# A transformer block on one core: value tiles through other staging rooms, background loads on ScalarE's queue, additions ordered behind weight halves

## The chip, the cores and the metric

The kernel runs on one core of one Trainium2 chip. The metric is the device time of one execution in microseconds (us); lower is better. Times of several executions are given as a median. The profile and the trace come from one further execution, which has a time of its own.

The engines are named as the profile does: PE is TensorE with its matmuls, PEld its weight loads, DVE is VectorE, ACT is ScalarE, POOL is GpSimd, SP is SyncE. Each engine works through its own list of instructions in order. DMAs are issued by SP, ACT or POOL and run on 16 DMA engines.

## The reference

One layer on a sequence of 1024 tokens with 1024 channels, everything in float32:

```python
h = rmsnorm(x, g_pre_mix)
proj = h @ w_in                       # u_pool | q | k | v, 512 channels each
y_pool = multiscale_pool(u_pool, ...) @ w_br_pool   # trailing means of 2, 4, 8, 16 tokens
o_sb = stick_breaking_attention(q, k, v)            # 8 heads of 64, strictly causal
gates = sigmoid(h @ w_gate + b_gate)  # 2048 channels
merged = gates[:, :1024] * y_pool + gates[:, 1024:] * (o_sb @ w_br_sb)
x = x + rmsnorm(merged @ w_out, g_post_mix)
h2 = rmsnorm(x, g_pre_mlp)
ff = square(relu(h2 @ w_up)) @ w_down  # 4096 channels between
x = x + rmsnorm(ff, g_post_mlp)
```

## The kernel before

Each float32 factor is split into a high and a low part of a reduced format. A product is then three matmuls of 128 x 512 (L104 high by high, L105 and L106 with one low part each) into one PSUM bank. Weights are split by `split_weights` (L1112 to L1119): a cast on ACT gives the high half, a subtraction on DVE (L1118) the low half; `prep` (L64) does the same with L74 and L75. TensorE needs both halves.

The program is a row of phases. The scheduler of the tile framework merges what the code issues into one list for each engine, and `issue_after` makes one instruction be placed behind another.

**Projection** (`phase_project`, L620). The gate, q and k projections are made as 12 pairs of outputs (L485: gates 0 to 4, q 0, k 0, q 1, k 1, gates 5 to 7). A pair is made with 7 products of 12 matmuls in place of 8, so there are 84 products, and the q and k pairs are products 35 to 62. The products go to PSUM banks of three tags in turn, with 2, 2 and 3 banks, so that 7 can be in flight (L626). DVE and ACT read the products and combine them in tiles u, c11, v and c22 (L651 to L662). When one of the four results of a pair is complete, `result` (L521) finishes it. For a gate, ACT takes the sigmoid (L526) and issues the store (L527). For q and k, ACT casts the high part (L530) and DVE computes the low part (L531) into a room in SBUF (128 x 1024 elements), and POOL issues the stores to DRAM: four for a q tile (L538 and L536 twice each), two for a k tile (L536). The rooms are m0 and m1 in turn (`staged`, L517). A room is free again when the last store from it has landed.

**In the background** of the same products runs the generator `later` (L540). Each `yield` in it waits for the next product (`next(bg)`, L638); every sixth product takes one step more (L640, L641). It first loads the pooling weights (L547), then makes four pooling groups in the rooms m0 to m3: a load of u (L555), running sums on DVE, a matmul `dm`, an evacuation on ACT (L584) and DVE, two stores (L590). Then come eight value tiles: two loads of 256 KB `vpair` (L595), a difference on DVE (L599), a cast on ACT (L602), a residual on DVE (L603), a store of 512 KB (L604). Tile t takes two neighbouring rooms, `vpair` in m2 and `vs` in m3 for even t, m0 and m1 for odd t.

**Attention** (`phase_attention`, L899) takes the q, k and value tiles back from DRAM. SP issues the loads of the first two heads into m0 to m3 (`load_head`, L705 to L718).

**Post** (`phase_post`, L968): the second half of the out projection runs on TensorE (L104 to L106 with `mg_hi`, `mg_lo`). Beside it, `chain(h=0)` (L1014) makes the norm of the first half of the tokens: for each of 8 blocks of channels a scaling on DVE (L1037), an addition of the residual (L1041), a store (L1042) and a square for the next norm. For the second half (h = 1) these two instructions are ordered behind the last low half of `prep` (`last_lo`); for h = 0 they aren't.

**MLP** (`phase_mlp`, L1150). A first loop makes 32 outputs and stores them (`pscr`). Then 16 pairs of outputs are made with 5 products each (L1194 on). For each pair the weights' sums and halves are made one pair ahead (`pair_weights`, L1139: L1126 to L1136 sums, L1118 low halves). Two quarters, u and c11, come back from `pscr` on ACT's queue (`quarter`, L1180), and DVE adds them (L1205) before ACT takes the squared ReLU (L1154, L1155) and POOL stores it (L1156).

Of the kernel before, what the change touches and what calls it, by code (L numbers as in the profile page):

```python
# [19 lines left out]
F32 = mybir.dt.float32  # L20
# [12 lines left out]
P = 128  # L33
# [19 lines left out]
class Block:  # L53
# [486 lines left out]
    def later(self):  # L540

        nc = self.nc
        def whole(n, dt=F32, name="ps"):
            return self.mx.tile([P, 1024], dt, name=name, tag=f"m{n}")

        wm = whole(0)[:, :512].rearrange("p (g n) -> p g n", g=4)
        nc.gpsimd.dma_start(wm, self.wmix)  # L547
        wmh, wml = (self.rp.tile([P, 4, P], F32R, name=f"wm{n}", tag=f"rb{n}") for n in range(2))
        nc.scalar.copy(wmh, wm)
        nc.vector.tensor_sub(wml, wm, wmh.bitcast(F32))  # L550
        yield
        for g in range(4):
            iu = 3 * (g % 2)
            u = whole(iu, name="u")
            nc.gpsimd.dma_start(u, self.uscr[g])  # L555
            yield
            yield
            yield
            cur, n = u, 0
            for i in range(g + 1):  # L560
                sh = 1 << i
                n = 1 + i % 2
                nxt = whole(n, name="win")
                nc.vector.tensor_add(nxt[:, sh:], cur[:, sh:], cur[:, : 1024 - sh])
                nc.vector.tensor_copy(nxt[:, :sh], cur[:, :sh])
                cur = nxt
                yield
            w = 1 << (g + 1)
            nc.vector.scalar_tensor_tensor(
                out=cur[:, w:], in0=cur[:, w:], scalar=1.0 / w, in1=u[:, w:], op0=ALU.mult, op1=ALU.subtract  # L570
            )
            nc.vector.tensor_mul(cur[:, :w], cur[:, :w], self.rcnt[:, :w])
            nc.vector.tensor_sub(cur[:, :w], cur[:, :w], u[:, :w])
            yield
            sc = self.vt[:, V_PSC + g : V_PSC + g + 1]
            ph, pq = whole(3 - n, F32R, "ph"), whole(3 - iu, F32R, "pq")
            nc.scalar.copy(ph, cur)
            nc.vector.tensor_sub(pq, cur, ph.bitcast(F32))
            yield
            for h in range(2):  # L580
                c = slice(h * H, h * H + H)
                d = self.zps.tile([P, H], F32, name="dm", tag="o", bufs=1)
                self.mm3(d, [(wmh[:, g, :], wml[:, g, :], ph[:, c], pq[:, c])])
                nc.scalar.activation(cur[:, c].bitcast(F32R), d, AF.Copy, scale=sc)  # L584
                nc.vector.scalar_tensor_tensor(
                    out=u[:, c].bitcast(F32R), in0=d, scalar=sc, in1=cur[:, c], op0=ALU.mult, op1=ALU.subtract
                )
                yield
            for t, scr in zip((cur, u), self.yscr):
                nc.gpsimd.dma_start(scr[:, g, :], t)  # L590
        for t in range(NK):
            n = 2 * (t % 2 == 0)
            p = self.mx.tile([P, 2, H], F32, name="vpair", tag=f"m{n}")
            for j in range(2):
                nc.gpsimd.dma_start(p[:, j, :], self.vscr[t * P + j : t * P + j + P, :])  # L595
            yield
            yield
            e = p[:, 0, :]
            nc.vector.tensor_sub(e, e, p[:, 1, :])  # L599
            e = e.rearrange("p (h x) -> p h x", h=8)  # L600
            v = self.mx.tile([P, 8, P], F32R, name="vs", tag=f"m{n + 1}")
            nc.scalar.copy(v[:, :, 0:64], e)  # L602
            nc.vector.tensor_sub(v[:, :, 64:128], e, v[:, :, 0:64].bitcast(F32))  # L603
            nc.gpsimd.dma_start(self.sscr[t], v.rearrange("p h x -> p (h x)").bitcast(F32))  # L604
            yield

    def sum_pieces(self, behind, n):
        with self.tc.issue_after(behind.ins):
            for _ in range(n):
                next(self.wsums)  # L610
# [9 lines left out]
    def phase_project(self):  # L620
        tc, nc = self.tc, self.nc
# [3 lines left out]
        def part(name):  # L625
            return pw.tile([P, H], F32, name=name, tag=name, bufs=1 + (name == "u"))  # L626
# [6 lines left out]
        def product(w, at, name):  # L633
            pool, tag, n = next(banks)
            d = pool.tile([P, H], F32, name="sw", tag=tag, bufs=n)
            self.half(d, w, at, name)
            next(nxt, None)
            next(bg, None)  # L638
            c = next(count)
            if c % 6 == 5:  # L640
                next(bg, None)  # L641
            if c % 2 and c < 32:
                self.sum_piece_with(self.last_mm)
            return d

        for i, (kind, f1) in enumerate(self.PAIRS):
# [3 lines left out]
            u, c11, v, c22 = (part(n) for n in ("u", "c11", "v", "c22"))  # L650
# [27 lines left out]
        for h in range(2):  # L678
            c = slice(h * H, h * H + H)
# [334 lines left out]
    def chain(self, ch, h, mix, acc):  # L1014

        nc = self.nc
        xr = []
        for i, n in enumerate(("hi", "lo")):
            t = self.hp.tile([P, 4, H], F32, name=f"xr{h}_{n}", tag=f"t4_{n}")
# [12 lines left out]
        for e in range(8):  # L1032
            yield 6 + 3 * e
            m = mix[e]

            with self.tc.issue_after(self.last_lo) if h else contextlib.nullcontext():
                nc.vector.scalar_tensor_tensor(  # L1037
                    out=m, in0=m, scalar=self.gn[:, V_POST_MIX + e : V_POST_MIX + e + 1], in1=r,
                    op0=ALU.mult, op1=ALU.mult,
                )  # L1040
                nc.vector.tensor_add(m, m, xr[e])  # L1041
            nc.gpsimd.dma_start(self.xscr[h][e], m)  # L1042
            sq = tmp[:, e % 3, :] if e else acc2
            nc.scalar.activation(sq, m, AF.Square)
            if e:
                nc.vector.tensor_add(acc2, acc2, sq)
# [16 lines left out]
        t = [self.big.tile([P, NK, H], F32R, name=f"b{h}_{n}", tag=f"big_{n}{h}") for n in ("hi", "lo")]  # L1063
# [48 lines left out]
    def split_weights(self, src, pool, tag, bufs, room=1024):  # L1112
        nc = self.nc
        n = src.shape[-1]
        hi = pool.tile([P, room], F32R, name=f"{tag}hi", tag=f"{tag}hi", bufs=bufs)[:, :n]
        lo = pool.tile([P, room], F32R, name=f"{tag}lo", tag=f"{tag}lo", bufs=bufs)[:, :n]
        nc.scalar.copy(hi, src)  # L1117
        nc.vector.tensor_sub(lo, src, hi.bitcast(F32))  # L1118
        return hi, lo  # L1119

    def pair_b(self, raw, sums, *where):
# [28 lines left out]
    def phase_mlp(self):  # L1150
        tc, nc = self.tc, self.nc
# [8 lines left out]
        for n, (i, j) in enumerate([(0, 0), (1, 0), (0, 1), (1, 1)] + [(i, j) for i in range(2, 16) for j in range(2)]):  # L1160
# [3 lines left out]
            t = self.ch.tile([P, H], F32, name="p1", tag="p1", bufs=3)  # L1164
# [12 lines left out]
        def buf(name):  # L1177
            return mp.tile([P, H], F32, name=name, tag="a", bufs=8)
# [12 lines left out]
        for i in range(16):  # L1191
# [10 lines left out]
            u, c11 = ps  # L1202
            ps = quarter(i + 1)
            v, c22 = buf("v"), buf("c22")
            nc.vector.tensor_add(c11, c11, u)  # L1205
            act_out(f1, 0, c11, c11)
            nc.vector.tensor_sub(u, u, product(w["sb"], 0, "t2"))
            nc.vector.tensor_sub(v, product(w["sa"], 0, "t3"), u)  # L1208
# [369 lines left out]
```

## Time and profile before

| | |
|---|---|
| median of 2 runs | 1348.27 us (1348.11 to 1348.43) |
| the profiled execution | 1346.78 us |
| its span, first to last instruction | 1345.1 us |
| mean granted TensorE clock | 0.978 |
| PE busy | 1261.2 us, 94% |
| DVE busy | 975.8 us, 73% |
| ACT busy | 626.4 us, 47% |
| POOL busy | 188.9 us, 14% |
| DMA moved | 283 MB, 210 GB/s on average |

The busy share of an engine is an average over phases that have different limits. PE busy includes matmuls that run at a lowered clock, so a stretch is better judged by how many matmuls it held. A row of waits gives the engine and line that waited, what released it, the total, the number of times and the longest.

### The profile page before, as it was taken

What the parts mean: (1) busy time and instruction counts of PE and PEld (TensorE: products, weight loads), DVE (VectorE), ACT (ScalarE), POOL (GpSimd) and SP (SyncE); (2) the same over time, 40 slices, a digit from 0 to 9 for tenths busy, and PEclk for the clock granted to TensorE, in tenths of its full rate; (3) what the DMA queues carried; (4) which work ended last, traced back from release to release, by engine and by line L of the source; (5) the groups of instructions that cost most, each with busy time, mean ns of one, the idle gap of its engine ahead of it and who ended that gap; (6) DMA issues with size and microseconds to landing.
All of it is one profiled execution on the core that took longest, in us unless ns stands there. A gap on an engine that the chain in (4) does not pass through costs nothing. (4 is left out here: it accounts for less than half of the span.)

```text
span 1345.1 us, 16167 instructions
## 1 busy us (share of the span) xinstructions
PE 1261.2 (94%) x5707; PEld 1032.5 (77%) x5707; DVE 975.8 (73%) x1311; ACT 626.4 (47%) x994; POOL 188.9 (14%) x336
## 2 busy tenths in 40 slices
PE   9998999685999988999899979999999999999998
PEld 6886887564877866887678868888778888888888
DVE  8657788665558899875787878777676565766985
ACT  7146343222435555664455655544455443343453
POOL 1302210243201101110001001211112110000000
PEclk9999999888999999999999989999999999999999
DMA  5576985586698866524566695755548998556561
GB/s 207 197 179 166 238 258 175 183 267 207 204 366 283 272 184 178 125 65 101 201 230 219 195 314 171 242 195 189 181 151 289 306 307 268 192 184 244 201 219 64
DMA packets 109218, 283.01 MB, mean 210 GB/s; under 512 B 12464, under 2 KB 17584, under 8 KB 107984
## 3 DMA queue, kind: packets, MB, share of 16 engines
q1 hardware_dynamic: 66272, 167.37, 36.1%
q0 software_dynamic: 32352, 95.59, 25.6%
q10 hardware_dynamic: 10512, 19.01, 4.5%
q8 instruction: 45, 0.74, 0.2%
q14 instruction: 37, 0.30, 0.1%
HBM read 208.52 MB, written 94.37 MB: 225 GB/s over the span
## 5 line engine op out<-in xcount | busy, mean ns | idle before, releaser
L105 PE MATMUL d<-blo,whi 128*128 128x512 f32 (+1 forms) x456 | 172.3, 378 | 0.0
L106 PE MATMUL d<-bhi,wlo 128*128 128x512 f32 (+1 forms) x456 | 171.9, 378 | 0.0
L104 PE MATMUL d<-bhi,whi 128*128 128x512 f32 (+1 forms) x456 | 168.7, 378 | 0.0
L105 PEld LDWEIGHTS d<-blo,whi 128*128 128x128 f32 x456 | 85.7, 188 | 16.1
L106 PEld LDWEIGHTS d<-bhi,wlo 128*128 128x128 f32 x456 | 85.8, 188 | 15.8
L104 PEld LDWEIGHTS d<-bhi,whi 128*128 128x128 f32 x456 | 85.5, 188 | 16.1
L747 DVE TENSOR_TENSOR_SCAN T<-T,past 128x768 f32<-128x768 f32 (+6 forms) x64 | 84.9, 1348 | 8.0 <-ACT T L745 7.9
L105 PE MATMUL d<-b_lo,whi 128*128 128x512 f32 x196 | 75.9, 389 | 0.0
L74 ACT CAST whi<-wraw 128x1024 fp32r<-128x1024 f32 x45 | 47.3, 1052 | 61.4 <-DMA wraw<-w 18.0
L104 PE MATMUL d<-b_hi,whi 128*128 128x512 f32 x196 | 75.1, 389 | 0.0
L106 PE MATMUL d<-b_hi,wlo 128*128 128x512 f32 x196 | 74.5, 389 | 0.0
L75 DVE TENSOR_TENSOR wlo<-wraw,whi 128x1024 fp32r<-128x1024 f32 x45 | 55.0, 1222 | 20.7 <-ACT whi L74 20.4
L770 ACT CAST ahi<-at 128x512 fp32r<-128x512 f32 (+1 forms) x96 | 45.2, 480 | 52.3 <-PE at L760 37.0
L771 DVE TENSOR_TENSOR alo<-at,ahi 128x512 fp32r<-128x512 f32 (+1 forms) x96 | 50.9, 548 | 20.1 <-ACT ahi L770 19.6
L104 PE MATMUL sw<-h_hi,whi 128*128 128x512 f32 x144 | 57.4, 399 | 7.6 <-DVE c L652 5.0
L1301 DVE TENSOR_TENSOR wlo<-slots_hi,whi 128x1024 fp32r<-128x1024 f32 x29 | 35.5, 1224 | 38.1 <-ACT whi L1299 37.9
L1299 ACT CAST whi<-slots_hi 128x1024 fp32r<-128x1024 f32 x29 | 30.5, 1051 | 66.4 <-PE d L105 60.3
L745 ACT ACTIVATE T<-z 128x256 f32<-128x256 f32 (+3 forms) x96 | 44.8, 496 | 29.6 <-PE z L743 16.1
L1299 ACT CAST whi<-slots_lo 128x1024 fp32r<-128x1024 f32 x27 | 28.4, 1053 | 61.7 <-PE d L105 51.2
L105 PE MATMUL sw<-h_lo,whi 128*128 128x512 f32 x144 | 57.0, 396 | 0.0
L104 PE MATMUL d<-t_hi,whi 128*128 128x512 f32 x132 | 52.7, 399 | 4.5 <-ACT whi L1117 4.5
L106 PE MATMUL sw<-h_hi,wlo 128*128 128x512 f32 x144 | 56.8, 396 | 0.0
(429 smaller groups left out, 3464.4 us busy)
## 6 DMA issues: line engine op xcount, KB each, us to landing
wraw<-w SPq DMA_DIRECT2D x57, 512.0 KB, 4.5
ext_b<-ascr SPq DMA_DIRECT2D x40, 512.0 KB, 7.0
wscr<-w POOLq DMA_DIRECT2D x32, 512.0 KB, 8.6
slots_hi<-w SPq DMA_DIRECT2D x10, 1024.0 KB, 8.4
slots_lo<-w SPq DMA_DIRECT2D x10, 1024.0 KB, 8.7
qq<-qscr SPq DMA_DIRECT2D x32, 256.0 KB, 6.1
gt<-gscr SPq DMA_DIRECT2D x32, 256.0 KB, 4.2
pscr<-p SPq DMA_DIRECT2D x32, 256.0 KB, 4.0
```

What stands on the lines that cost most here:

```text
L74: nc.scalar.copy(hi, raw)
L75: self.last_lo = nc.vector.tensor_sub(lo, raw, hi.bitcast(F32)).ins
L104: nc.tensor.matmul(ps, wh, rh, start=first and i == 0, stop=False)
L105: nc.tensor.matmul(ps, wh, rl, start=False, stop=False)
L106: self.last_mm = nc.tensor.matmul(ps, wl, rh, start=False, stop=last and i == n - 1).ins
L745: self.after = nc.scalar.activation(f, z[:, :n], AF.Sigmoid, scale=-1.0)
L747: nc.vector.tensor_tensor_scan(f[:, ::-1], f[:, ::-1], past[:, ::-1], 1.0, ALU.mult, ALU.max)
L770: nc.scalar.copy(hi[:, c:], at[:, c:])
L771: nc.vector.tensor_sub(lo[:, c:], at[:, c:], hi[:, c:].bitcast(F32))
L1299: last_split[0] = nc.scalar.copy(hi, src).ins
L1301: last_split[1] = nc.vector.tensor_sub(lo, src, hi.bitcast(F32)).ins
```

## The change

Four things are changed, and nothing in what is computed.

1. In `later`, the loads of the pooling weights, of u and of the value pairs are issued by ACT where POOL issued them.
2. The value tiles 0 to 4 and 6 all take m2 and m3; tiles 5 and 7 take m0 and m1. A tile waits three products between its loads and its difference where it waited two, and tiles 0 to 4 are followed by two more steps. The step that every sixth product takes more ends at product 36. The tiles thus spread over some 40 products where they took some 20.
3. In `chain`, the scaling and the addition of the first half are also ordered behind `last_lo`.
4. `split_weights` remembers its last low half in `last_split`, and the addition of the two quarters in the MLP's pair loop is ordered behind it.

```diff
         wm = whole(0)[:, :512].rearrange("p (g n) -> p g n", g=4)
-        nc.gpsimd.dma_start(wm, self.wmix)
+        nc.scalar.dma_start(wm, self.wmix)
...
             u = whole(iu, name="u")
-            nc.gpsimd.dma_start(u, self.uscr[g])
+            nc.scalar.dma_start(u, self.uscr[g])
...
         for t in range(NK):
-            n = 2 * (t % 2 == 0)
+            n = 0 if t in (5, 7) else 2
             p = self.mx.tile([P, 2, H], F32, name="vpair", tag=f"m{n}")
             for j in range(2):
-                nc.gpsimd.dma_start(p[:, j, :], self.vscr[t * P + j : t * P + j + P, :])
+                nc.scalar.dma_start(p[:, j, :], self.vscr[t * P + j : t * P + j + P, :])
+            yield
             yield
             yield
...
             nc.gpsimd.dma_start(self.sscr[t], v.rearrange("p h x -> p (h x)").bitcast(F32))
             yield
+            if t < 5:
+                yield
+                yield
...
-            if c % 6 == 5:
+            if c % 6 == 5 and c < 36:
                 next(bg, None)
...
-            with self.tc.issue_after(self.last_lo) if h else contextlib.nullcontext():
+            with self.tc.issue_after(self.last_lo):
...
-        nc.vector.tensor_sub(lo, src, hi.bitcast(F32))
+        self.last_split = nc.vector.tensor_sub(lo, src, hi.bitcast(F32)).ins
...
-            nc.vector.tensor_add(c11, c11, u)
+            with tc.issue_after(self.last_split):
+                nc.vector.tensor_add(c11, c11, u)
```

The change has four more lines ahead of `chain` than the kernel before, so L1037 is L1041 there, L1118 is L1122, and L1205 is L1210; inside `later` L595 stays, and L602 to L604 are L603 to L605.

How the lists of the engines change is shown at three places. The first is the value tiles among the q and k results. POOL's list before, from the k and q stores (`qscr`), the loads of value pairs (`vpair`) and the stores of value tiles (`sscr`):

```order
L604 DMA sscr_141<-vs 128x1024
L595 DMA vpair<-vscr 128x512 x2
L538 DMA qscr_4_128<-qs 64x512
L538 DMA qscr_5_129<-qs 64x512
L536 DMA qscr_4_128<-qs 64x2x512
L536 DMA qscr_5_129<-qs 64x2x512
L595 DMA vpair<-vscr 128x512 x2
L604 DMA sscr_143<-vs 128x1024
L595 DMA vpair<-vscr 128x512 x2
L604 DMA sscr_144<-vs 128x1024
```

and ACT's list after the change, where the last pooling group is evacuated (`win<-dm`) and the first value tiles follow:

```order
L584 ACTIVATE win<-dm,vt 128x512
L530 ACTIVATE qs<-c_1859 128x512
L1121 CAST a0hi<-wrawx 128x512
L595 DMA vpair<-vscr 128x512 x2
L1121 CAST s0hi<-wraw 128x1024
L530 ACTIVATE qs<-u 128x512
L1121 CAST whi<-wrawx 128x1024
L655 COPY u<-sw 128x512
L603 CAST vs<-vpair 128x8x64
L595 DMA vpair<-vscr 128x512 x2
L530 ACTIVATE qs<-v 128x512
```

The loads of value pairs have left POOL's list, which keeps the stores; they stand in ACT's, each behind the cast of the value tile before (L603), with casts of weights, of q and copies of products behind them.

The second place is in post: DVE's list before, from the first scaling of the norm of the first half (`mix_0` to `mix_3` hold two channel blocks each, `xr` is the residual, `wlo` the low half of an out weight):

```order
L1037 SCALAR_TENSOR_TENSOR mix_0_4721<-mix_0_4721,gn,ny 128x512 x2
L1037 SCALAR_TENSOR_TENSOR mix_1_4722<-mix_1_4722,gn,ny 128x512 x2
L1037 SCALAR_TENSOR_TENSOR mix_2_4723<-mix_2_4723,gn,ny 128x512 x2
L1037 SCALAR_TENSOR_TENSOR mix_3_4724<-mix_3_4724,gn,ny 128x512 x2
L1041 TENSOR_TENSOR mix_0_4721<-mix_0_4721,xr_hi 128x512 x2
L1041 TENSOR_TENSOR mix_1_4722<-mix_1_4722,xr_hi 128x512 x2
L75 TENSOR_TENSOR wlo<-wraw,whi 128x1024
```

and after:

```order
L1041 SCALAR_TENSOR_TENSOR mix_0_4721<-mix_0_4721,gn,ny 128x512 x2
L1041 SCALAR_TENSOR_TENSOR mix_1_4722<-mix_1_4722,gn,ny 128x512 x2
L1045 TENSOR_TENSOR mix_0_4721<-mix_0_4721,xr_hi 128x512 x2
L1045 TENSOR_TENSOR mix_1_4722<-mix_1_4722,xr_hi 128x512 x2
L75 TENSOR_TENSOR wlo<-wraw,whi 128x1024
L1041 SCALAR_TENSOR_TENSOR mix_2_4723<-mix_2_4723,gn,ny 128x512 x2
```

Four of the eight scalings now stand behind the first weight half.

The third place is the start of the MLP's pair loop: DVE's list before, where the sums of the first pair's weights end and its halves are made (`wlo`), with the additions of the quarters (`u<-u`):

```order
L1126 TENSOR_TENSOR sums<-wraw 128x512
L1135 TENSOR_TENSOR sums<-wraw 128x512
L1136 TENSOR_TENSOR sums<-wraw 128x512
L1127 TENSOR_TENSOR sums<-wraw,sums 128x512
L1205 TENSOR_TENSOR u<-u 128x512
L1128 TENSOR_TENSOR sums<-wraw,sums 128x512
L1205 TENSOR_TENSOR u<-u 128x512
L1118 TENSOR_TENSOR wlo<-sums,whi 128x1024
L1118 TENSOR_TENSOR wlo<-wraw,whi 128x512
L1118 TENSOR_TENSOR wlo<-sums,whi 128x1024
```

and after:

```order
L1131 TENSOR_TENSOR sums<-wraw,sums 128x512
L1132 TENSOR_TENSOR sums<-wraw,sums 128x512
L1122 TENSOR_TENSOR wlo<-sums,whi 128x1024
L1122 TENSOR_TENSOR wlo<-wraw,whi 128x512
L1122 TENSOR_TENSOR wlo<-sums,whi 128x1024
L1130 TENSOR_TENSOR sums<-braw 128x512
L1139 TENSOR_TENSOR sums<-braw 128x512
L1140 TENSOR_TENSOR sums<-braw 128x512
L1131 TENSOR_TENSOR sums<-braw,sums 128x512
L1132 TENSOR_TENSOR sums<-braw,sums 128x512
L1122 TENSOR_TENSOR slo<-sums,shi 128x1024
L1122 TENSOR_TENSOR wlo<-sums,whi 128x1024
```

No addition of quarters stands between the sums and the halves of the first pair any more; the first one follows three rows further down, behind the halves of the second pair.

## The prediction

> **What bounds the kernel now.** I read the busy shares first, then windows of TensorE, then the waits of the windows that fall short, then the lengths of the single steps there. The page's head, and three windows (time, then busy time and count for PE, PEld, DVE, ACT, POOL, then granted clock, DMA share, GB/s):
>
> ```profile
> span 1345.1 us, 16167 instructions
> 250.00:350.00 100.00, 68.21 (x260) 53.54 (x259) 58.80 (x84) 29.76 (x43) 42.02 (x74) 0.85 0.75 234
> 840.00:880.00 40.00, 40.00 (x178) 33.11 (x177) 31.40 (x47) 21.01 (x33) 8.07 (x15) 1.00 0.70 233
> ```
>
> The third row is TensorE at full speed: 178 matmuls in 40 us, 0.2247 us each, the rate against which I measure every other stretch. At it, 100 us hold 445. The stretch 250 to 350, in which the q and k pairs are made, has 260, so 185 × 0.2247 = 41.6 us are lost there: 31.8 us stand still, the rest is a lower clock (0.85 granted against 1.00). The waits of that stretch (total, times, longest):
>
> ```profile
> POOL vpair L595 <- PE dm L106: 28.3, 1, 28.3
> POOL sscr L604 <- DVE vs L603: 21.7, 6, 8.8
> PE sw L104 <- DVE v L655: 20.9, 3, 11.9
> ACT qs L530 <- DMA sscr<-vs: 7.7, 3, 4.8
> PE sw L104 <- ACT u L651: 5.9, 2, 3.4
> PE sw L104 <- DVE c L652: 5.0, 2, 4.6
> ```
>
> TensorE waits for evacuations (L651, L652, L655: 31.8 us in 7 waits), so for PSUM banks. The evacuating engines aren't full (DVE 58.8 of 100 us, ACT 29.8); they stand behind instructions of their own queue, and the fourth row names one: ScalarE's cast L530 into a staging room waits for a store of a value tile, which held that room. So the two rooms m0 and m1 are the suspects. Whether they set the length can be counted from the steps that hold a room:
>
> ```profile
> L536 POOL DMA_DIRECT2D qscr<-qs x16 | 9.6, 602 | 2.4 <-DVE qs L531 2.3
> L595 POOL DMA_DIRECT2D vpair<-vscr x16 | 9.0, 567 | 34.9 <-PE dm L106 28.3 <-DMA yscr<-win 2.0 <-issue 2.0
> L538 POOL DMA_DIRECT2D qscr<-qs x16 | 8.5, 538 | 4.2 <-ACT qs L530 3.9
> L536 POOL DMA_DIRECT2D qscr<-ks x14 | 8.4, 601 | 12.6 <-DVE ks L531 12.6
> L604 POOL DMA_DIRECT2D sscr<-vs x8 | 4.5, 560 | 21.8 <-DVE vs L603 21.7 <-issue 0.2
> L599 DVE TENSOR_TENSOR vpair<-vpair 128x512 f32<-128x512 f32 x8 | 5.5, 690 | 15.3 <-DMA vpair<-vscr 15.3
> L602 ACT CAST vs<-vpair 128x512 fp32r<-128x512 f32 x8 | 5.0, 619 | 15.6 <-DVE vpair L599 15.0 <-DMA qscr<-qs 0.7
> L603 DVE TENSOR_TENSOR vs<-vpair,vs 128x512 fp32r<-128x512 f32 x8 | 5.5, 689 | 2.2 <-ACT vs L602 2.1
> L530 ACT ACTIVATE qs<-c 128x512 fp32r<-128x512 f32 x4 | 2.5, 627 | 2.8 <-DVE vs L603 1.8 <-DMA sscr<-vs 0.9
> ```
>
> and the landings (issue to landing, last column):
>
> ```profile
> vpair<-vscr POOLq DMA_DIRECT2D x16, 256.0 KB, 5.7
> qscr<-qs POOLq DMA_DIRECT2D x16, 256.0 KB, 5.2
> sscr<-vs POOLq DMA_DIRECT2D x8, 512.0 KB, 4.4
> qscr<-ks POOLq DMA_DIRECT2D x14, 256.0 KB, 3.7
> ```
>
> A q tile holds its room for cast 0.63, residual 0.69, four issues 2 × (0.538 + 0.602) = 2.28 and landing 5.2: 8.8 us. A k tile with two issues: 0.63 + 0.69 + 1.20 + 3.7 = 6.2 us. The four pairs make 8 of each, taken by m0 and m1 in turn, so 4 × (8.8 + 6.2) = 60 us for each room. In the kernel before, the odd value tiles come on top: m0 takes the pair load, 1.13 + 5.7 + 0.69 + 0.62 + 0.69 = 8.8 us, four times, together 95; m1 takes 0.62 + 0.69 + 0.56 + 4.4 = 6.3, four times, together 85. The trace, from the first q cast to the last k cast:
>
> ```profile
> 252.34 0.62 ACT L530 ACTIVATE qs<-c 128x512 fp32r<-128x512 f32 x1
> 349.16 0.63 ACT L530 ACTIVATE ks<-u 128x512 fp32r<-128x512 f32 x1
> ...
> 350.44 0.33 ACTq L527 DMA_DIRECT2D gscr<-c  x1
> ```
>
> 97 us, against 95 counted for m0: the room m0 sets this stage. (The last row, a load or store issued on ScalarE, serves below.) TensorE's own need is 28 products of 12 matmuls, 28 × 12 × 0.2247 = 75.5 us.
>
> **The change part by part.**
>
> *Rooms and spread of the value tiles.* Tiles 0 to 4 and 6 now go through m2 and m3, which only the pooling groups used; 5 and 7, left in m0 and m1, come after the last k tile. That leaves 60 us per room against 75.5 us of matmuls, and TensorE becomes the bound with 15 us in hand. One tile per room m2/m3 each six products (16.2 us) against 8.8 us of holding is no bound either. Bounds of the gain: at most the whole 41.6. At the other end the stores land at their slowest:
>
> ```profile
> DMA to landing us min/median/max: 2.2/4.5/6.7
> DMA to landing us min/median/max: 2.9/3.7/6.8
> ```
>
> (first q, then k). With 6.7 and 6.8 a q tile holds 10.3 and a k tile 9.3 us. Results come at products 2, 5, 6 and 7 of a pair, so u takes c22's room 2 products (5.4 us) later and the next pair's first takes v's 3 products (8.1 us) later: waits of 4.9 + 2.2 for q and 3.9 + 1.2 for k, over two pairs each 24 us. If the PSUM banks in hand hide none of it, the gain is 41.6 − 24 = 17. At the median landings the same sum gives 3.4 + 0.7 for q and 0.8 for k, 10 us over the four pairs, and a result can be several products late before the banks run out, so most is hidden; I take 5 us as left over: **−37**, between −42 and −17.
>
> *The queue.* 16 pair loads, four u loads and wmix leave POOL's queue. That frees 16 × 0.567 = 9 us of issuing on an engine that is busy 42 of 100 us, and takes out of its row the wait of 28.3 us for a pooling group's last matmul, behind which q stores would stand. On ScalarE each pair load now waits in order until its two rooms are free. In the new order each stands right behind the cast L603 of the tile before, whose only later reader is one DVE step of 0.69 us, so w = 1 to 2 us each; only the first waits for the last pooling store (an estimate from the store landings above and their slowest, 5 to 9 us), and tile 5 for k stores, some 4. Sum about 20 us on an engine with 70 of 100 us free: nothing, if copies L651/L655 are not queued behind; that is in the 5 us above. The Trainium skill, page "DMA: Bandwidth & Descriptors", section "Issuing engines are not separate DMA queues", states that loads started by different engines share the same 16 DMA engines and that a second issuer saves only issue time: by it this part alone is worth those 9 us at most, and no transfer gets shorter. No row here contradicts it; the rooms carry my sum, not the queue.
>
> *Into attention.* The last value tile now leaves m0/m1 at the end of the stage, and head 0 is loaded into these rooms. The window behind it, and SP's longest wait:
>
> ```profile
> 380.00:400.00 20.00, 17.49 (x85) 14.59 (x84) 11.69 (x17) 6.19 (x13) 1.08 (x2) 1.00 1.04 400
> SPq L718 <- DMA qscr<-ks: 35.3, 1, 35.3
> ```
>
> DMA is full there at 400 GB/s. Two 512 KB stores and one pair load more before head 0 are 1.3 MB, 3.3 us; part is hidden under the last g products: **+2**, 0 to +6.
>
> *First norm's additions (post).*
>
> ```profile
> 660.00:680.00 20.00, 12.96 (x37) 10.04 (x38) 18.55 (x28) 8.62 (x14) 4.40 (x8) 0.74 0.53 188
> PE d L106 <- DVE wlo L75: 5.1, 1, 5.1
> L1037 DVE SCALAR_TENSOR_TENSOR mix<-mix,gn,ny 128x512 f32<-128x512 f32 x8 | 5.4, 753 | 0.0
> ```
>
> TensorE waits 5.1 us for a weight half that stands on DVE behind eight scalings (8 × 0.675 us in sequence) and four additions. Now four scalings and four additions stand ahead: 4 × 0.675 = 2.7 us earlier. What is late next are channels 2 and 3 of that half, whose norm has all of the first MLP loop as cover. The window holds 37 matmuls of a possible 89, so more than 2.7 could come back if the clock stays up: **−3**, −1 to −7.
>
> *The MLP's additions.* The pair loop starts with these rows (TensorE's, then DVE's):
>
> ```profile
> 780.00:820.00 40.00, 32.57 (x131) 25.89 (x130) 27.65 (x41) 19.31 (x31) 3.24 (x6) 0.87 0.77 252
> 796.24 0.80 PE L104 MATMUL d<-t_hi,whi 128*128 128x512 f32 x1 [4.45 <-ACT whi L1117]
> 800.44 0.79 PE L106 MATMUL d<-t_hi,wlo 128*128 128x512 f32 x1 [2.98 <-DVE wlo L1118]
> 793.82 0.69 DVE L1205 TENSOR_TENSOR u<-u 128x512 f32<-128x512 f32 x1 [3.23 <-DMA u<-pscr]
> 798.56 0.69 DVE L1205 TENSOR_TENSOR u<-u 128x512 f32<-128x512 f32 x1 [3.45 <-DMA u<-pscr]
> ```
>
> (178 − 131) × 0.2247 = 10.6 us are lost. Both additions wait for a load (3.23 and 3.45 us) with the weight sums and halves behind them. In the new order the first addition follows the pair's last half, so 6.7 us of waiting and 1.4 of additions leave the path: **−8**, at most −10.6, at least −5 if the first half is then late by its own loads. The addition's reader is the ReLU of that quarter, and its store, which no product waits for.
>
> Later in the loop:
>
> ```profile
> 960.00:1000.00 40.00, 35.94 (x154) 28.17 (x153) 28.09 (x41) 19.42 (x30) 7.00 (x13) 1.00 0.58 193
> DVE u L1205 <- DMA u<-pscr: 28.6, 12, 4.4
> ```
>
> (178 − 154) × 0.2247 = 5.4 us lost while DVE waits 28.6 us over the loop at these additions: **−3**, 0 to −5.
>
> **The sum**: −37 + 2 − 3 − 8 − 3 = −49. The profiled execution took 1346.78 us (span 1345.1 and 1.7 around it), so 1297.8; the median of the runs, 1348.27, lies 1.5 higher: **1299 us**.
>
> **The rivals.**
>
> *Late landings* (the two rooms still bound): stores as slow as the slowest above, nothing hidden: −17 instead of −37, so 1319. For it: DMA share 0.75 here already, and the value traffic is now spread over more products. Against: the pair loads no longer compete for these rooms.
>
> *The MLP's additions give nothing*: DVE's other steps delay the halves as long; without the −8 and −3, 1310. For it: DVE is busy 28 of 40 us there. Against: the rows show idle DVE.
>
> *Late into attention*: head 0 waits the full stores behind the stage, +10 instead of +2, 1307. For it: DMA at 400 GB/s at 380 to 400.
>
> *Only the queue counts*: the rooms were not the bound, and the gain there is the 9 us of issuing: 1299 + 28 = 1327. This is also what the skill's rule would leave. Against: 95 counted and 97 measured.
>
> *ScalarE blocked, the slow side*: ScalarE runs its queue in order, and each pair load holds it for w. With 29.8 us of work and 16 × 0.33 us of issue (the L527 row), 35 together, eight loads make the stage 35 + 8w; from w = 5 it passes TensorE's 75.5, from w = 10 the kernel is slower than before (stage 115, the 15 lost against 14 won elsewhere). At w = 12 the stage is 131: 31 − 12 gives 1367. For it: the wait of 28.3 us moves to ScalarE if the first pair load is reached early. Against: the order puts it behind the pooling group's own evacuation, so that wait occurs once and is short.
>
> **How the numbers follow.** Forecast 0.60, late landings 0.13, MLP nothing 0.10, late into attention 0.10, only the queue 0.04, ScalarE blocked 0.03. The forecast's own bounds are 1287 (−42, 0, −7, −10.6, −3, nearly all at once) and 1311; to leave no more than 2 in 10 out the range goes on to the late landings and the queue: 1286 to 1326. A measurement of this kernel can tell about 2%, 27 us, from no change, so faster means under 1321. The forecast, MLP nothing, late into attention and half of the late landings lie there: with a little off for their spread 0.86; same 0.11; slower 0.03.
>
> **What would show it** (lines as numbered before)**.** Right: the q/k stage, first q cast to last k cast, takes 76 to 82 us instead of 97, and TensorE's waits for L655 there fall from 20.9 to under 5; no cast of q waits for a store of a value tile; the wait for wlo L75 halves; in the MLP's start the two gaps of 4.45 and 2.98 are gone, and the additions L1205 no longer wait for u. Wrong: a stage over 90 us with q and k casts waiting for qscr (late landings); ScalarE idle over 5 us at each L595; TensorE's first attention matmuls idle over 5 us for kk or qq; the weight halves in the MLP as late as now.

## The result, and the profile after

| | before | after |
|---|---|---|
| median | 1348.27 us (2 runs) | 1315.16 us (2 runs, 1314.89 to 1315.42) |
| ratio, 95% interval | | 0.9754, 0.9712 to 0.9796 |
| span of the profiled execution | 1345.1 us | 1313.7 us |
| mean granted clock | 0.978 | 0.988 |

The change saves 33 us, 2.5%. The forecast was 1299: the direction and the range held, and 16 us of the gain are missing. Measured a second time, the same kernel took 1318.19 us, at 0.9802 (0.9787 to 0.9816), so about 2% is what to count on.

Where the time came from is read best from one table. Every execution here issues the same number of matmuls in nearly the same order, so the time at which the Nth matmul starts can be set against that of the kernel before. A difference that grows in a stretch was won or lost there (us, negative is ahead of the kernel before):

| matmul | up to here the program has done | after | the change once more |
|---|---|---|---|
| 480 | input phase, first gate products | −0.2 | 0.1 |
| 780 | gates 0 to 3, pooling beside them | 12.9 | 13.1 |
| 1020 | gate 4, products of q 0 and k 0 (their casts lag behind) | 11.0 | 11.2 |
| 1320 | q 1, k 1, gate 5 and half of gate 6 | −21.3 | −21.0 |
| 1620 | last gates, first scores of attention (“into attention”) | −12.9 | −14.5 |
| 2640 | attention | −14.0 | −13.1 |
| 3000 | post, first MLP matmuls | −16.1 | −16.0 |
| 3300 | first MLP loop, start of the pair loop | −26.3 | −26.3 |
| 4200 | pair loop | −31.6 | −31.7 |
| 5700 | end | −31.6 | −31.7 |

Two stretches lose time, and the prediction had nothing for the first (13 us) and 2 us for the second (8.4 us).

The stage of the q and k pairs, first the window that lost 41.6 us before:

```profile
250.00:350.00 100.00, 94.19 (x402) 76.80 (x402) 69.13 (x100) 36.10 (x52) 36.18 (x63) 0.97 0.83 268
```

and the waits there:

```profile
POOL qscr L538 <- ACT qs L530: 38.5, 6, 25.9
...
DVE vpair L600 <- DMA vpair<-vscr: 9.7, 6, 3.4
...
ACT qs L530 <- DMA qscr<-qs: 5.1, 3, 2.1
...
PE sw L104 <- DVE v L659: 4.8, 1, 4.8
```

402 matmuls in place of 260. TensorE's wait for L655 (now L659) fell from 20.9 to 4.8 us, and a q cast now waits for stores of q (5.1 us) or of k (1.8 us), never for one of a value tile. The casts themselves, with the first and the last start (two views, of the q tile and of the k tile):

```profile
L530 ACT ACTIVATE qs<-c x4: 620/630/634, 254.3 to 297.7; 128x512 fp32r<-128x512 f32 x4
```

```profile
L530 ACT ACTIVATE ks<-v x2: 632/632/632, 289.4 to 331.7; 128x512 fp32r<-128x512 f32 x2
```

From 254.3 to 332.3 the stage takes 78 us, where 76 to 82 were predicted and 97 stood before. But it starts 2 us later than before.

### The profile page after: what moved, and what is told of

Its sections match the earlier page's. It is cut to its first block, busy times and chain, and to the rows that moved or that the text cites. A ratio compares the mean times of both kernels' runs of the same rounds, so it can differ in the third digit from the quotient of the medians.

```text
span 1313.7 us, 16195 instructions
## 1 busy us (share of the span) xinstructions
PE 1255.1 (96%) x5707; PEld 1027.8 (78%) x5707; DVE 972.6 (74%) x1311; ACT 623.0 (47%) x994; POOL 177.5 (14%) x315
## 4 chain that ended last, share of the span: by engine, by line
PE 71%; DMA 10%; DVE 8%; issue 6%; ACT 3%; POOL 1%; ACTq 0%; SPq 0%; DVEq 0%; POOLq 0%
PE d L106 16%; PE d L104 16%; PE d L105 16%; PE sw L104 2%; PE sw L105 2%; PE sw L106 2%; PE o L790 2%; PE dbr L105 2%; PE dbr L102 2%; PE dbr L106 2%; PE at L764 2%; DMA qscr<-qs 1%; DMA vscr<-ev 1%; DMA yscr<-win 1%; DMA gt<-bscr 1%
## 5 line engine op out<-in xcount | busy, mean ns | idle before, releaser
L104 PEld LDWEIGHTS d<-bhi,whi 128*128 128x128 f32 x456 | 85.5, 188 | 16.1
L1121 ACT CAST whi<-wraw 128x1024 fp32r<-128x1024 f32 (+1 forms) x29 | 26.9, 930 | 56.4 <-PE du L105 10.1
```

Source lines behind the costliest of these rows:

```text
L104: nc.tensor.matmul(ps, wh, rh, start=first and i == 0, stop=False)
```

## The experiments

Each kernel was measured beside the kernel before, on the same chip. The runs of the kernel before lay between 1340 and 1352 us there, wider than the two runs of the first measurement, so ratios with their intervals are given, and the stretches are compared in the traces, as in the table above. A trace is one execution, and its time can lie some us from the median; where that bears on a reading, it is said.

**The loads of the pooling weights and of u back on POOL.** The early loss shows in the changed kernel as two waits on DVE, between 125 and 185 us:

```profile
DVE win L564 <- DMA yscr<-win: 12.0, 1, 12.0
ACT ph L577 <- DVE win L573: 10.3, 1, 10.3
...
DVE win L564 <- DMA u<-uscr: 4.9, 1, 4.9
```

In DVE's timeline the running sum waits first, and a weight half and a difference of products stand right behind it:

```profile
133.29 1.22 DVE L564 TENSOR_TENSOR win<-u 128x1023 f32<-128x1023 f32 x1 [4.88 <-DMA u<-uscr]
134.44 0.14 DVE L565 COPY win<-u 128x1 f32<-128x1 f32 x1
134.50 1.21 DVE L1122 TENSOR_TENSOR wlo<-wraw,whi 128x1024 fp32r<-128x1024 f32 x1
...
172.61 1.22 DVE L564 TENSOR_TENSOR win<-u 128x1023 f32<-128x1023 f32 x1 [11.97 <-DMA yscr<-win]
173.75 0.14 DVE L565 COPY win<-u 128x1 f32<-128x1 f32 x1
173.82 0.68 DVE L658 TENSOR_TENSOR u<-u,sw 128x512 f32<-128x512 f32 x1
```

and TensorE stops for them:

```profile
135.77 0.50 PE L106 MATMUL sw<-ht_hi,wlo 128*128 128x512 f32 x1 [3.10 <-DVE wlo L1122]
...
178.76 0.80 PE L104 MATMUL dm<-ph,wm 128*128 128x512 f32 x1 [3.71 <-ACT ph L577]
```

In the list of DVE these two sums stand 8 and 12 rows earlier than before. They do so with the queue alone too (below), and not with the five loads on POOL's queue; that the scheduler expects u earlier from ScalarE is the likely reason, which was not looked into. The edit:

```diff
-        nc.scalar.dma_start(wm, self.wmix)
+        nc.gpsimd.dma_start(wm, self.wmix)
-            nc.scalar.dma_start(u, self.uscr[g])
+            nc.gpsimd.dma_start(u, self.uscr[g])
```

> The change, with the loads of the pooling weights and of u back on POOL's queue; the value pairs stay on ScalarE's. Theory: these five loads make the pooling groups' running sums move forward in DVE's list, ahead of weight halves (row 122 in place of 130 for the first group, 153 in place of 165 for the second), where they wait for data (4.9 and 12.0 us in the trace); the kernel loses 13 us between the 480th and the 780th matmul by it. With the list as before, 1315 - 13 = 1302 us. Rival, a loss by the DMA traffic or by the spread of the value tiles: 1315 us.

Measured: 1327.74 us, 0.9861 (0.9821 to 0.9901), slower than the change and not faster. The early loss is gone as expected (0.8 in place of 12.9 at the 780th matmul), and yet at the 1320th this kernel is 21.0 us ahead, just as the change is (21.3). The q and k stage loses in its first part what was saved before:

```profile
256.29 0.79 PE L104 MATMUL sw<-h_hi,whi 128*128 128x512 f32 x1 [5.23 <-DVE c L656]
265.85 0.50 PE L104 MATMUL sw<-ht_hi,whi 128*128 128x512 f32 x1 [2.05 <-ACT u L655]
275.23 0.80 PE L104 MATMUL sw<-ht_hi,s1hi 128*128 128x512 f32 x1 [4.81 <-DVE v L659]
```

The reason for the first wait stands in ScalarE's timeline of this kernel: the first two q casts come right around the last evacuation of the last pooling group (L584). Its operands ph and pq lie in m1 and m0, the rooms that the casts need, till its last matmul `dm` has read them; that matmul starts at 250.7 us.

```profile
252.29 0.63 ACT L530 ACTIVATE qs<-c 128x512 fp32r<-128x512 f32 x1
252.83 0.67 ACT L584 ACTIVATE win<-dm,vt 128x512 fp32r<-128x512 f32 x1
253.40 0.62 ACT L530 ACTIVATE qs<-c 128x512 fp32r<-128x512 f32 x1
259.77 2.40 ACTq L595 DMA_DIRECT2D vpair<-vscr  x2
262.22 1.05 ACT L1121 CAST whi<-wrawx 128x1024 fp32r<-128x1024 f32 x1 [8.20 <-issue]
```

So the start of the stage was set by the pooling groups, not by TensorE: first q cast at 252.3 us before, 254.3 after, 252.3 here, each behind the last `dm` (250.2, 254.1, 250.7). The last two rows show something more: behind these casts ScalarE stands still for 8.2 us. The first pair load waits there for the pooling group's store out of m2, and the next casts and the copy L655, for which TensorE waits at 265.85, stand behind it. That is the blocking of ScalarE that the prediction had as a rival, in this experiment and not in the change. The theory of where the 13 us go was right, that they cost 13 us in the end was wrong. The rest of the difference to the change lies behind attention, in code that the edit doesn't touch: the start of the MLP's pair loop won 5 us here, 10 there, and post lost 1.4 us here where the change won 2.1.

**All loads on ScalarE, each running sum behind the last weight half.**

```diff
-                nc.vector.tensor_add(nxt[:, sh:], cur[:, sh:], cur[:, : 1024 - sh])
-                nc.vector.tensor_copy(nxt[:, :sh], cur[:, :sh])
+                with self.tc.issue_after(self.last_split):
+                    nc.vector.tensor_add(nxt[:, sh:], cur[:, sh:], cur[:, : 1024 - sh])
+                    nc.vector.tensor_copy(nxt[:, :sh], cur[:, :sh])
```

> The change, with all loads left on ScalarE's queue, and each running sum of the pooling groups ordered behind the last weight half. Theory of the place in DVE's list: 1302 to 1304 us, and no wait over 3 us of a running sum ahead of a weight half. Rival, that ScalarE's queue is itself what loses the time, by waiting in order for rooms: 1315 us as with the change.

Measured: 1329.44 us, 0.9874 (0.9839 to 0.9908). At the 780th matmul 4.5 us are lost in place of 12.9, with the same queue, so most of the early loss is the place of the sums in DVE's list. But the kernel is only 10.6 us ahead at the 1320th matmul, and the expected time was missed again. The first q cast comes at 254.9, about as in the change, and the last k cast at 341.8 in place of 331.7, so here it is the stage itself that is longer. ScalarE's first pair load waits 7.4 us again, and TensorE then waits 9.97 us once for L660 (4.8 in the change); that the one makes the other was not tested.

**The rooms and the spread alone**, all loads on POOL:

```diff
-            n = 2 * (t % 2 == 0)
+            n = 0 if t in (5, 7) else 2
...
+            yield
...
+            if t < 5:
+                yield
+                yield
...
-            if c % 6 == 5:
+            if c % 6 == 5 and c < 36:
```

> The kernel before with the value tiles' rooms and their spread alone, all loads left on POOL. Theory that the rooms carry the gain of the q and k stage (34 us) and the later last tile the loss into attention (8): 1348 - 34 + 8 = 1322 us. Rival, that the queue carries it (pair loads that wait on POOL hold the q and k stores behind them): 1335 to 1348 us.

Measured: 1338.93 us, 0.9946 (0.992 to 0.9971), between the two. At the 1260th matmul it is 21.1 us ahead (the change 23.0), so the rooms carry the gain of the q and k stage by themselves. Then it loses 29 us: it is 8.2 us behind at the 1500th. (The execution of this trace took 1347.13 us, the longest of ten, against a median of 1338.93, so most of them lose less.) TensorE's longest wait there, and SP's:

```profile
PE z L744 <- issue: 12.3, 1, 12.3
```

```profile
SPq L721 <- DMA vpair<-vscr: 17.7, 1, 17.7
```

On POOL the last pair load is issued at 359.6 us, on ScalarE at 343.1. In POOL's list the last pair load stands behind the store of the tile before, which waits 10.2 us there for its residual (L604), and head 0's loads wait on SP for the rooms of the last tile. The last k cast comes later as well (339.6 us, 331.7 in the change). That is what ScalarE's queue is good for in this change: not for the stage, but for the tiles behind it.

**The queue alone**, rooms and spread as before:

```diff
-        nc.gpsimd.dma_start(wm, self.wmix)
+        nc.scalar.dma_start(wm, self.wmix)
-            nc.gpsimd.dma_start(u, self.uscr[g])
+            nc.scalar.dma_start(u, self.uscr[g])
-                nc.gpsimd.dma_start(p[:, j, :], self.vscr[t * P + j : t * P + j + P, :])
+                nc.scalar.dma_start(p[:, j, :], self.vscr[t * P + j : t * P + j + P, :])
```

> The kernel before with all the background loads on ScalarE's queue, rooms and spread as before. Theory that the rooms set the stage: nothing won there, up to 13 us lost early by the running sums' place in DVE's list, 1348 to 1361 us. Rival, that the queue carries the gain of the stage: 1348 - 34 + 13 = 1327 us.

Measured: 1347.71 us, 1.0007 (0.9982 to 1.0032): nothing. The early 12.8 us are lost as in the change, 7 come back by the 1320th matmul. The q casts begin at 255.1 and the last k cast at 357.6, 103 us: the two rooms set the stage as long as the odd value tiles share them. The rival that the queue carries the gain (1327) is out.

**The change once more.**

> The change itself once more, so that the other runs of this call stand beside it on one chip. 1315 us; its stretches within 1 us of the first trace up to the end of attention, and whatever differs behind that is what executions differ by.

Measured: 1318.19 us, 0.9802 (0.9787 to 0.9816); its column in the table agrees with the first trace within 1.7 us everywhere. So the stretches repeat from one execution to another; both traced ones took 1315 us.

**Less spread.** The end of the projection in the changed kernel:

```profile
364.82 0.47 PE L104 MATMUL dbr<-yhi,whi 128*128 128x512 f32 x1 [1.68 <-DMA yhi<-yscr]
...
368.74 0.50 PE L105 MATMUL dbr<-ylo,whi 128*128 128x512 f32 x1 [2.06 <-DMA ylo<-yscr]
376.15 0.50 PE L104 MATMUL dbr<-yhi,whi 128*128 128x512 f32 x1 [2.18 <-DVE gt L854]
386.46 0.77 PE L744 MATMUL z<-kk,qq 128*128 128x512 f32 x1 [3.00 <-issue]
```

```profile
360.00:380.00 20.00, 14.07 (x60) 10.56 (x59) 4.38 (x7) 3.28 (x7) 1.09 (x2) 1.00 1.02 377
```

TensorE waits for y, which is loaded behind the loads of head 0, while DMA is full (share 1.02). Two causes are possible. The first edit lets the tiles come earlier:

```diff
             if t < 5:
                 yield
-                yield
```

> The change with one extra step behind value tiles 0 to 4 in place of two, so that the last value tile leaves its rooms some five products (13.5 us) earlier. Theory: the 8.4 us that the change loses between the end of the projection and the first scores come from the last value tile, behind which SP's loads of head 0 and of y stand; most of them come back, 1308 us. Rival, that DMA is full there anyway (1.02 share, 377 GB/s at 360 to 380 us): 1315 us, unchanged.

Measured: 1323.31 us, 0.9825 (0.9796 to 0.9855). The way into attention (1320th to 1620th matmul) costs 2.1 us in place of 8.4, as the theory says, but 13.8 us are lost just ahead of it:

```profile
330.20 0.50 PE L104 MATMUL sw<-h_hi,whi 128*128 128x512 f32 x1 [4.58 <-DVE c L655]
344.97 0.79 PE L104 MATMUL sw<-ht_hi,s0hi 128*128 128x512 f32 x1 [5.59 <-DVE v L658]
```

Value tile 5 now takes m0 and m1 among the last k tiles, and the last k cast comes at 346.7 where it came at 331.7. This is the old stall again, made by one tile.

**Value tile 5 through m2 and m3 too**, on top of less spread:

```diff
-            n = 0 if t in (5, 7) else 2
+            n = 0 if t == 7 else 2
```

> The run before with less spread, and value tile 5 through m2 and m3 too, so that m0 and m1 hold nothing but q and k tiles until the last k tile is cast. Theory: with less spread alone tile 5 came among the k tiles and cost 13.8 us between the 1260th and the 1320th matmul; that goes, the better way into attention (2 us lost in place of 8) stays: 1318 - 6 = 1312 us. Rival, that the faster pace of tiles through m2 and m3 or the DMA traffic made the 13.8 us: 1323 us, unchanged.

Measured: 1320.07 us, 0.9796 (0.9749 to 0.9843). Between the 1260th and the 1320th matmul 6.6 us are lost in place of 13.8 (16.1 ahead at the latter), and the way into attention costs 3.5 us. So tile 5 was half of it; what the other half is was not followed up. At the 1620th matmul it stands at −12.5, where the change has −12.9: what is won on the way is lost ahead of it, and the way into attention ends at nearly the same time, 411 us, in both.

**One more gate pair ahead of q and k**, on top of the last kernel:

```diff
-    PAIRS = [("g", i) for i in range(5)] + [("q", 0), ("k", 0), ("q", 1), ("k", 1)] + [("g", i) for i in range(5, 8)]
+    PAIRS = [("g", i) for i in range(6)] + [("q", 0), ("k", 0), ("q", 1), ("k", 1)] + [("g", i) for i in range(6, 8)]
```

> The same kernel with one gate pair more ahead of the q and k pairs (gates 0 to 5, q and k, gates 6 and 7), so that the first q result comes 7 products (19 us) later while the pooling groups end at the same time. Theory: the q and k stage can't start before the last pooling group leaves its rooms, at 252 to 254 us in four kernels; here the first q result comes when they are free, so the 7.6 us lost between the 1020th and the 1080th matmul go, and the stage ends without other loss: 7 us less at the 1320th matmul than without the shift. The later k tiles may cost some of it on the way into attention: 1305 to 1312 us. Rival, that the stage's start is held by something that moves with the pairs (weights, the banks): the same loss 19 us later, 1312 us or more.

Measured: 1312.49 us, 0.9759 (0.9717 to 0.9801), in the profiled execution 1307.96. The window of the stage, and the one behind it:

```profile
240.00:340.00 100.00, 100.00 (x443) 82.81 (x442) 72.64 (x103) 36.83 (x52) 34.44 (x60) 1.00 0.76 248
345.00:375.00 30.00, 20.13 (x66) 14.71 (x64) 8.85 (x12) 6.33 (x9) 3.42 (x6) 0.83 1.01 363
```

TensorE doesn't wait at all from 240 to 340 us. At the 1320th matmul the kernel is 34.4 us ahead, 18.3 more than without the shift (expected were 7). Of the 18.3, 7.9 come between the 1020th and the 1080th matmul, where the theory has the wait for the pooling groups; 3.8 are won before, and 6.6 behind, where the unshifted kernel loses them for a reason that was not found. So the wait for the pooling groups goes when q comes later, as expected, and the shift does something else besides. Of the 34.4 us, 13.6 are given back on the way into attention, where DMA is full (1.01). The trace is of the shortest of four executions and that of the kernel without the shift of the longest of four: the medians differ by 7.6 us, the traces by 16.4. By its ratio this kernel can't be told from the change.

**Half of y ahead of head 0**, on top of the change: the loads of y for the first half of the tokens are written ahead of `load_head`, and four of them now stand ahead of head 0's k load in SP's list, where one did.

```diff
+        self.load_y(0)
         for h in range(2):
             self.load_head(h, 0, self.mx)
```

> The change with the first half of the loads of y written ahead of the loads of the first heads; in SP's list four loads of y then stand ahead of head 0's k load, where one did. Theory: on the way into attention the change loses 8.4 us because the loads of y wait on SP behind that k load, which waits for the last value tile's store (issued at 358 us, TensorE wants y at 363): the waits of 1.7 and 2.1 us for y go, and some of the clock, 1318 - 4 = 1314 us. Rival, that DMA is simply full from 350 to 390 us: what y wins the heads lose, 1318 us.

Measured: 1319.16 us, 0.9804 (0.9767 to 0.9842), the same as the change. Of the two waits for y (1.68 and 2.06 us) one of 1.21 is left, and the gate behind them takes most of the difference (3.89 us, 2.18 in the change):

```profile
366.70 0.50 PE L105 MATMUL dbr<-ylo,whi 128*128 128x512 f32 x1 [1.21 <-DMA ylo<-yscr]
375.78 0.79 PE L104 MATMUL dbr<-yhi,whi 128*128 128x512 f32 x1 [3.89 <-DVE gt L856]
386.55 0.47 PE L746 MATMUL z<-kk,qq 128*128 128x512 f32 x1 [2.62 <-issue]
```

The theory of the order falls here, as far as this edit goes: three loads of y are issued some 5 us earlier, head 0's first q loads still stand ahead of them, and the wait only moves. That fits the rival (DMA share 1.05 from 360 to 380 us).

**The shifted pairs, with the loads of the pooling weights and of u on POOL** (the edit of the first experiment).

> The kernel with the q and k pairs one gate pair later, and the loads of the pooling weights and of u back on POOL's queue. Theory: with the unshifted pairs the early loss of 13 us cost only 1 to 2 us, since the q and k stage waited for the last pooling group in any case; with the shifted pairs the stage no longer waits for it, so the early loss (8.7 us there) counts: 5 to 8 us less at the 1320th matmul than with the loads on ScalarE, and less of it at the end, since the way into attention is full of DMA: 1306 to 1311 us. Rival, that the last pooling group again ends too late (its matmul stands at place 1044 in TensorE's list, 970 to 1000 with the loads on ScalarE): the stage loses what the early part wins, 1312 us or more.

Measured: 1328.96 us, 0.99 (0.9842 to 0.9957). The rival holds. The early loss is gone (2.2 at the 780th matmul), but the first q cast comes at 256.4 in place of 251.0, the last k cast at 369.5 in place of 347.7, and of 33.7 us at the 1260th matmul nothing is left at the 1620th. With the shifted pairs the early loads on ScalarE's queue pay: they put stalls into the gates, and end the pooling groups sooner (last `dm` at 250.8 us against 255.4).

**The MLP's additions alone.**

```diff
-        nc.vector.tensor_sub(lo, src, hi.bitcast(F32))
+        self.last_split = nc.vector.tensor_sub(lo, src, hi.bitcast(F32)).ins
...
-            nc.vector.tensor_add(c11, c11, u)
+            with tc.issue_after(self.last_split):
+                nc.vector.tensor_add(c11, c11, u)
```

> The kernel before with the MLP's additions behind the weight halves alone. Theory: the 10.3 us of the loop's start and the 5.5 of its middle are all its doing, 16 us, 1346 - 16 = 1330 us. Rival, that part of it came from the loads' timing, which the earlier parts shift: a run with the same MLP code won 5 us at the start in place of 10, so 1335 to 1341 us.

Measured: 1332.41 us, 0.9902 (0.9878 to 0.9926), 12 us below the median of the kernel before beside it; in the trace 8.7 us are won at the start of the pair loop and 5.6 in its middle.

**The first norm's order in post alone.**

```diff
-            with self.tc.issue_after(self.last_lo) if h else contextlib.nullcontext():
+            with self.tc.issue_after(self.last_lo):
```

> The kernel before with the first norm's scalings and additions behind the out weights' halves alone. Theory: 5 us are won in post and 4 given back at the MLP's first matmul, which then waits for its first operand b_hi (2.40 us, then a lowered clock), since that operand needs this norm: 1346 - 1 = 1345 us, with the wait for b_hi in the trace, which the kernel before doesn't have. Rival, as predicted, the norm has cover: no wait for b_hi, 1341 to 1343 us.

Measured: 1345.9 us, 1.0006 (0.9987 to 1.0024): nothing, as the theory had it. 4.2 us are won between the 2640th and the 2880th matmul and 4.7 lost by the 2940th:

```profile
672.82 0.79 PE L106 MATMUL d<-mg_hi,wlo 128*128 128x512 f32 x1 [3.96 <-DVE wlo L75]
705.52 0.73 PE L104 MATMUL d<-b_hi,whi 128*128 128x512 f32 x2 [2.40 <-ACT b_hi L1011]
```

The second row, the MLP's first matmul waiting for its operand, is not in the kernel before; it is in the change (2.40 us at 686.78).

## Why the prediction was right and where it failed

*The bound.* Right. The two rooms set the q and k stage. The queue alone leaves it at 103 us, the rooms alone bring it to 83 us, and the change to 78 us, against 60 us of holding and 75.5 us of matmuls.

*"I take 5 us as left over"*: the step that failed. Up to the 1320th matmul 21.3 us were won and not 37. The 41.6 us lost before were all laid to the value tiles. A part of them was never theirs, and the trace of the kernel before shows it. The first q result is complete when DVE adds it up, the first q cast follows, and only then TensorE's first wait in that window ends (timelines of DVE, ScalarE and TensorE):

```profile
217.66 0.68 DVE L652 TENSOR_TENSOR c<-u,sw 128x512 f32<-128x512 f32 x1
```

```profile
252.34 0.62 ACT L530 ACTIVATE qs<-c 128x512 fp32r<-128x512 f32 x1
```

```profile
255.14 0.80 PE L104 MATMUL sw<-h_hi,whi 128*128 128x512 f32 x1 [4.56 <-DVE c L652]
```

The result lay there for 34 us while the pooling groups held m0 and m1. I measured the stage from its first cast on, and took the gain from a window in which TensorE also paid for the late start. The two numbers of the prediction don't agree: a stage of 76 to 82 us in place of 97 is 15 to 21 us shorter, and the sum took 37. The stage became 19 us shorter, near the 21.3 us won. The first q cast moves from 252 to 254 us in the change, and the first q result lies for 25 us. With q later (the shifted pairs) it lies for 7 us, and 34.4 us are won by the 1320th matmul. That is near the forecast of 37, but only in part for this reason, as said there.

*"Nothing" for the queue.* Half right. In the change no copy or cast of the stage stood long behind the pair loads. But the five loads of the pooling phase were costed with the others, and what they do was missed: they move other instructions in DVE's list, which costs 13 us of stalls among the gates. Of the change's own bill that is nearly neutral, since the stage waited for the pooling groups anyway: undone, 0.3 us less are won at the 1320th matmul. The Trainium skill's rule in "DMA: Bandwidth & Descriptors", "Issuing engines are not separate DMA queues", holds for the queue alone, which changed nothing (1.0007). It doesn't hold for the change as a whole, where the pair loads on POOL cost 21 us by the 1500th matmul (the rooms alone, 8.2 behind, against the first experiment, 12.9 ahead; up to there only the queue of the pair loads differs, and the first of the two traces is of a long execution): a queue is also a place in an engine's order.

*Into attention*: +2 was predicted with up to +6, and it was +8.4; the rival of 10 us was nearer. The reason named there, the last tile's traffic, is only part of it: earlier tiles cut the loss to 2 to 3.5 us, but with tile 5 moved as well the scores began at nearly the same time. DMA at full share (1.02 at 360 to 380 us, 1.01 at 345 to 375 with the shifted pairs) is the simplest account of both, and putting y first fits it. It was not tested by itself, and it can't be all: the kernel before had 1.04 at 380 to 400 us and made 85 matmuls there, where the change made 60 from 360 to 380. The cause stays open.

*Post*: −3 predicted, −2.1 in the change and +0.5 alone. The wait for the weight half fell by 1 us (5.1 to 4.0) and not by half, and "whose norm has all of the first MLP loop as cover" was wrong: the MLP's first operand is made from that norm.

*The MLP*: −8 and −3 predicted, −10.2 and −5.3 measured. The row of the additions shows it, before (780 to 1000 us) and after (760 to 1000 us):

```profile
L1205 DVE TENSOR_TENSOR u<-u 128x512 f32<-128x512 f32 x16 | 11.1, 694 | 35.2 <-DMA u<-pscr 35.2
```

```profile
L1210 DVE TENSOR_TENSOR u<-u 128x512 f32<-128x512 f32 x16 | 10.9, 684 | 0.0
```

No idle time is left ahead of them. Both terms were taken too small: nearly the whole loss that the prediction had counted (10.6 and 5.4 us) came back. At the loop's start that is more than the two gaps (7.4 us), since the granted clock there rose from 0.87 to 1.00; in the middle it was 1.00 before as well.

*The rivals.* Late landings: the longest q landing did grow (8.2 us in the change, 6.7 before), and the q and k casts still wait 16.5 us in all for stores of q and k; yet the stage took 78 us, and TensorE stood still for 5.8 us of it. ScalarE blocked: not in the change, where the first pair load is issued 3.3 us after ScalarE's last cast; in the first two experiments it waited 8.2 and 7.4 us.

*The total.* That it lies within the range is partly luck. The rooms gave 15.7 us less than the sum had and the way into attention took 6.4 more, while the MLP gave 4.5 more; and the range went up to 1326 for late landings and the queue, neither of which is what held the gain back.

Left open: in several kernels with the same MLP code (the first experiment, and tile 5 moved) the start of the pair loop won 5 us in place of 10. There TensorE waits 3 us for a cast behind weight sums. What makes them later was not followed up.

## What to carry to other kernels

A stage that waits for a buffer has a length and a start, and each has its own cause: ask when the first result was ready, and who held the buffer until then, before the whole loss is laid to one user of it. Moving a load to another queue changes more than the load: look at every engine's order, since the scheduler moves the load's readers too, and here it put sums that wait up to 12 us ahead of weight halves. An edit that takes one instruction out of the way puts another behind: who reads it is the first thing to look up, as the norm in post showed.

## What was not expected of the hardware

The store of the first pooling group (512 KB, `yscr<-win`) took 16.9 us to land in the change, the longest of eight whose median is 8.8; it is the one that DVE waits 12 us for. An issue can take much longer than usual: two pair loads on ScalarE's queue took 2.40 us to issue in the first experiment, where one issue takes 0.33 us elsewhere. DMA was full there (share 1.03 from 259 to 263 us); that this is the reason was not tested.
